# Moving the 1/rms of Q from the softmax scale onto Q itself

## The chip, the cores and the metric

The kernel runs on one core of one Trainium2 chip. The metric is the device time of one execution in microseconds (us). The kernel before takes 629.34 us, the median of three runs (629.11 to 629.71).

A core has five instruction streams that run at once and meet only at semaphores: TensorE (PE, matmuls, with its weight loads PEld), VectorE (DVE), ScalarE (ACT), GpSimd (POOL) and SyncE (SP, which here only issues transfers). Each engine executes its own instructions strictly in the order in which they were queued: an instruction that waits holds everything behind it on the same engine.

## The reference

One layer of a hybrid encoder, 512 tokens of width 2048, all in float32. What matters here is the attention half:

```python
proj = einsum('bsd,de->bse', rms_norm(x, norm_w), w_in)
q, k, v, g_attn, xr, g_lru = split(proj)
q = rms_norm(q.reshape(B, S, 8, 128), q_norm_w)      # per head: q / rms(q) * w
k = rms_norm(k.reshape(B, S, 2, 128), k_norm_w)
q, k = apply_axial_rope(q), apply_axial_rope(k)       # a rotation of pairs of columns
s = (q @ k.T) * 128 ** -0.5                           # per head, 4 query heads share one k
p = softmax(s);  out = p @ v
```

Beside it runs a gated linear recurrence (LRU) over the same tokens. Both halves are normed, gated with silu, joined and multiplied by `w_out`, and the input is added. Since the rotation acts on each token's row linearly, the factor 1/rms of a token and head may be applied before the rotation, after it, or to that token's row of the scores: the result is the same up to rounding.

## The kernel before

Every large product is made of three matmuls (`mm3`, lines 155 to 158): each float32 operand is split into a high part (ACT copies it to a rounded type, `wh`, line 231) and a low part (DVE subtracts, `wl`, line 232), and PE adds high·high, high·low and low·high. A projection goes through `w_in` in chunks of 256 rows by 512 columns (`wload`): SP loads a chunk into a ring of three, ACT and DVE split its two halves, and PE uses the pair for 24 matmuls. `xh` and `xl` hold the split, transposed input.

The order of the stages is: LRU projections and the LRU itself; the projection of K and V with the second half of the LRU; the two projections of Q, four heads each (`both`, `q_proj`, lines 1366 to 1376); then attention (`attention`, line 824), woven into the projections of the gates (`gates`); the last gate; the output projection (`outputs`).

After a Q projection, `evac_tok` (line 645) copies four tiles of 128 tokens by 512 columns out of PSUM, each scaled by the token's input norm. `norm_rope` (line 659) then does, per tile `t`, on ACT four squares with sums (line 670), on POOL the power -1/2 of the mean (`rsqrt_mean`, lines 377 and 378), and on DVE the rotation: two half products with the sines (line 678), the product with the cosines (line 684), the sum (line 685). For K the norm is multiplied in ahead of the rotation (line 676). For Q it is not: the 1/rms values go to a constant table `qscale` of 128 tokens by 2 groups by 4 tiles by 4 heads. `sent` transposes the rotated tiles in blocks on DVE and sends them through DRAM; `landed` and `turned` bring a head back transposed and split it (`q`, line 715).

In the attention, step `i` is head `h = i // 4`, query tile `t = i % 4`. `weights` (line 755) multiplies (scores in a PSUM bank), takes the negated row maximum on DVE (`mx`, line 766), multiplies it by `qscale` on ACT (line 768), exponentiates the scores on ACT with `qscale` as the scale and `mx` as the bias (line 770), takes the reciprocal of the row sums on DVE (line 771), divides on POOL (line 772) and transposes in blocks on DVE (`u`, line 773). Two steps make a half; `moved` sends it through DRAM (lines 781 and 788) and splits what comes back into `ph` (ACT) and `pl` (DVE), both line 792. `values` (line 795) multiplies with V some steps later.

What sets the order: PE's queue is written by hand from line 1222 on (`manual_schedule`), SP's within the attention as well. DVE, ACT and POOL are ordered by a planner at build time: it plays the program through with its own durations and queues, of the instructions ready at that moment, the one with the highest priority; program order is the priority, and `tc.high_priority(AHEAD)` moves the splits of weights and line 768 far ahead. What it queued is fixed on the chip. `STEPS`, `BEGIN` and `LATE` set how many quarters of a chunk PE works on between two steps of the attention.

Of the kernel before, what the change touches and what calls it, by code (L numbers as in the profile page):

```python
# [11 lines left out]
F32 = mybir.dt.float32  # L12
F32R = mybir.dt.float32r
AF = mybir.ActivationFunctionType
# [3 lines left out]
P = 128  # L18
# [3 lines left out]
NT = SEQ // P  # L22
HD = 128
NH = 8
NKV = 2
G = NH // NKV
# [10 lines left out]
AHEAD = 600  # L37
# [22 lines left out]
C_Q, C_K, C_GA, C_XR, C_GL = 0, 1024, 1536, 2560, 3584  # L60
# [6 lines left out]
def hybrid_kernel(  # L67
# [20 lines left out]
    nc = tc.nc  # L88
# [4 lines left out]
    pools, order = {}, {"left": [], "right": []}  # L93
# [27 lines left out]
    def nm(s):  # L121
        cnt[0] += 1
        return f"{s}_{cnt[0]}"
# [10 lines left out]
    def at(tag, bufs, shape, dt=F32):  # L134
        return pools["att"].tile([P, *shape], dt, tag=tag, bufs=bufs, name=nm(tag))
# [10 lines left out]
    def mm():  # L146
        return ps.tile([P, SEQ], F32, tag="mm", name=nm("mm"))

    def const(shape, name, dt=F32):
        return cp.tile(list(shape), dt, tag=name, name=name)  # L150
# [4 lines left out]
    def mm3(acc, lh, ll, rh, rl, start, stop):  # L155
        nc.tensor.matmul(acc, lh, rh, start=start, stop=False)  # L156
        nc.tensor.matmul(acc, lh, rl, start=False, stop=False)  # L157
        nc.tensor.matmul(acc, ll, rh, start=False, stop=stop)  # L158
# [96 lines left out]
    def behind(those):  # L255
        stack = ExitStack()
        for ins in those:
            stack.enter_context(tc.issue_after(ins))
        return stack
# [115 lines left out]
    def rsqrt_mean(dst, src, n, width):  # L375

        nc.gpsimd.tensor_scalar(dst, src, 1.0 / n, EPS, op0=ALU.mult, op1=ALU.add)
        last_pool[0] = nc.gpsimd.tensor_tensor(dst, dst, nhalf[:, :width], op=ALU.pow).ins
# [77 lines left out]
    def proj_tok(c0, acc, early=0):  # L456
        yield from tok_block(acc, w_in, 0, c0, xh, xl, KT, early)
# [7 lines left out]
    def drain(fill):  # L465
        for _ in fill:
            pass
# [177 lines left out]
    def evac_tok(acc, tile_of):  # L645

        res = []
        with tc.high_priority():
            for t in range(NT):
                e = tile_of()  # L650
                evacs[:] = [
                    nc.scalar.activation(e, acc[t], AF.Identity, scale=rstd[:, t : t + 1]).ins
                ]
                res.append(e)
        return res

    qscale = const([P, NKV, NT, G], "qscale")

    def norm_rope(es, nh, tab, home, n="", those=(), scales=()):

        es = [e[:, : nh * HD].rearrange("p (h d) -> p h d", d=HD) for e in es]
        rs = []
        for e in es:
            r = scales.pop(0) if scales else pools[home].tile(
                [P, nh], F32, tag=f"rr{n}", bufs=NT, name=nm("rr")
            )
            for h in range(nh):
                sq = pools[home].tile([P, HD], F32, tag=f"sh{n}", bufs=1, name=nm("sh"))
                with behind(those):
                    nc.scalar.activation(sq, e[:, h, :], AF.Square, accum_out=r[:, h : h + 1])  # L670
            rsqrt_mean(r, r, HD, nh)
            rs.append(r)
        for t, (e, r) in enumerate(zip(es, rs)):
            sq = pools[home].tile([P, nh, HD], F32, tag=f"sq{n}", bufs=2, name=nm("sq"))
            if home == "rope":
                nc.vector.tensor_mul(e, e, r[:, :, None].broadcast_to([P, nh, HD]))
            for s in range(2):
                nc.vector.tensor_mul(
                    sq.rearrange("p h (a s d) -> p h a s d", s=2, d=32)[:, :, :, s, :],
                    e.rearrange("p h (a s d) -> p h a s d", s=2, d=32)[:, :, :, 1 - s, :],  # L680
                    tab[:, t, 1, :].rearrange("p (a s d) -> p a s d", s=2, d=32)[:, None, :, s, :]
                    .broadcast_to([P, nh, 2, 32]),
                )
            nc.vector.tensor_mul(e, e, tab[:, t, 0, :][:, None, :].broadcast_to([P, nh, HD]))
            nc.vector.tensor_add(e, e, sq)
        return es

    kth, ktl = [None] * NKV, [None] * NKV
# [56 lines left out]
    qs = {}  # L745

    def turned(h):

        q = at("q", 2, (2, SEQ), F32R)
        qs[h] = q[:, 0, :], q[:, 1, :]  # L750
        split_head(pairs[h // 2], h % 2, *qs[h])

    pts, summed = {}, []

    def weights(h, t, turned_, first=()):

        (qh, ql), g = qs[h], h // G
        scale = qscale[:, g, t, h % G : h % G + 1]
        tt = slice(t * P, (t + 1) * P)
        sc = mm()  # L760
        mm3(sc, qh[:, tt], ql[:, tt], kth[g], ktl[g], True, True)
        mx, sm = (at(n, 6, (1,)) for n in ("mx", "sm"))
        with ExitStack() as stack:
            for ins in first:
                stack.enter_context(tc.issue_after(ins))
            nc.vector.tensor_reduce(mx, sc, axis=AX.X, op=ALU.max, negate=True)
            with tc.high_priority(AHEAD):
                nc.scalar.activation(mx, mx, AF.Identity, scale=scale)
            p = at("p", 3, (SEQ,))
            nc.scalar.activation(p, sc, AF.Exp, bias=mx, scale=scale, accum_out=sm)  # L770
        nc.vector.reciprocal(sm, sm)  # L771
        last_pool[0] = nc.gpsimd.tensor_scalar(p, p, sm, 0.0, op0=ALU.mult, op1=ALU.add).ins  # L772
        nc.vector.transpose(  # L773
            turned_[:, :, :, t % 2, :].rearrange("p a s c -> p s a c"),
            p.rearrange("p (s a c) -> p s a c", a=NQ, c=B),
        )

    def moved(turned_, half, his):

        aside_ = dram.tile([P, NQ, NT * H // NQ], F32, name=nm("pd"), tag="pd", bufs=2 * NH)  # L780
        nc.sync.dma_start(aside_, turned_.rearrange("p a s t c -> p a (s t c)"))
        yield
        if half == 0:
            his += [at(n, 1, (NT, 2, NQ, H // NQ), F32R) for n in ("ph", "pl")]
        pt = at("pt", 2, (NQ, NT, H // NQ))
        src = aside_.rearrange("(i r) a x -> a r i x", r=B)
        for a in range(NQ):
            nc.sync.dma_start(  # L788
                pt[a * B : (a + 1) * B].rearrange("p i s x -> p i (s x)"), src[a]
            )  # L790
        hi, lo = (v[:, :, half].rearrange("p s i x -> p i s x") for v in his[:2])
        his += [nc.scalar.copy(hi, pt).ins, nc.vector.tensor_sub(lo, pt, f(hi)).ins]  # L792
        yield
# [25 lines left out]
    pairs, rot = [], []  # L819

    def next_pair():
        pairs.append(landed(asides.pop(0)))

    def attention():

        with tc.high_priority(AHEAD):
            for h in range(2):
                turned(h)
        yield BEGIN
        writes = []  # L830
        last, units = NH * NT, {}
        for i in range(last + NT + LATE):
            h, t = divmod(i, NT)
            if i < last:
                if t % 2 == 0:
                    u = at("u", 4, (NQ, NT, 2, B))
                first = pts[h - 2][2 + 2 * t : 4 + 2 * t] if h > 1 and t < 2 else ()
                weights(h, t, u, first)
                if t == 0 and 0 < h < NH - 1:
                    turned(h + 1)  # L840
                if t % 2:
                    units[i] = moved(u, t // 2, pts.setdefault(h, []))
            for j in (i - 1, i - 3):
                if j in units:
                    next(units[j])
            if i < 2:
                es = [e[:, 2 * i : 2 * i + 2] for e in rot]
                writes.append(sent(es, 2, at("u", 4, (NQ, 2, NT, B))))
                next(writes[i])
            elif i < 4:  # L850
                drain(writes[i - 2])
            if t == 2 and h % 2 and asides:
                next_pair()
            j = i - NT - LATE
            if j >= 0 and j % NT == NT - 1:
                hi, lo, *summed[:] = pts.pop(j // NT)
                values(j // NT, hi, lo)
            yield STEPS + (last <= i < last + NT)
# [381 lines left out]
    with tc.high_priority():  # L1240
# [6 lines left out]
        first = []  # L1247
# [103 lines left out]
    rq, rk = rope_consts()  # L1351
# [13 lines left out]
    opened("qkv", "right")  # L1365
    def q_proj(c0, acc):
        yield from proj_tok(c0, acc)
        g = (c0 - C_Q) // (G * HD)
        rot[:] = norm_rope(
            evac_tok(acc, ev), G, rq, "rot", scales=[qscale[:, g, t] for t in range(NT)]  # L1370
        )

    def both():
        yield from q_proj(C_Q, a4)
# [58 lines left out]
    with tc.manual_schedule(engines={mybir.EngineType.SP}):  # L1433
        weave(fill, attention())
# [41 lines left out]
    acc = []  # L1476
# [28 lines left out]
    last = ExitStack()  # L1505
# [47 lines left out]
```

## Time and profile before

| | us |
|---|---|
| median of three runs | 629.34 (629.11 to 629.71) |
| the profiled execution | 629.78 |
| its span, first to last instruction | 628.0 |
| PE busy | 622.1 (99%), 2740 matmuls |
| DVE busy | 490.0 (78%), 778 instructions |
| ACT busy | 370.4 (59%), 678 instructions |
| POOL busy | 106.4 (17%), 141 instructions |

A span of 628.0 us plus 1.78 us around it is the profiled execution's own time. A row of a timeline gives the start (us from the span's start), the duration (us), the engine, the line of the kernel, the operation, what it writes and reads, and, in brackets, the idle time ahead of it with what ended it. A row of a source view gives count and the least, median and greatest duration (ns).

### The profile page before, as it was taken

To read this page: it belongs to the slowest core of one execution; us is meant where nothing else is said; L and a number is where in the kernel's file an instruction comes from. 1 tells how busy PE (TensorE), PEld (TensorE's weight loads), DVE (VectorE), ACT (ScalarE), POOL (GpSimd) and SP (SyncE) were. 2 spreads that over 40 slices of the span, in tenths; PEclk is the share of its full clock that TensorE was granted. 3 is DMA by queue.
4 is the path that set the end of the run, shared out by engine and by line. 5 is a ranking of instruction groups with operands and counts; after the bars stand their busy time and mean duration, and the time that the engine had idled before them with its cause. 6 is when DMAs were issued, how large, how long until landed. Compare 5 with 4: busy or idle time off the path is not lost.

```text
span 628.0 us, 8301 instructions
## 1 busy us (share of the span) xinstructions
PE 622.1 (99%) x2740; PEld 510.9 (81%) x2740; DVE 490.0 (78%) x778; ACT 370.4 (59%) x678; POOL 106.4 (17%) x141
## 2 busy tenths in 40 slices
PE   9999999999999999999999999999999999999997
PEld 7888888888888888888878888888888888888886
DVE  6875878997798957777787888549987865986885
ACT  4586689959964825555585658337445543444441
POOL 3001111112040433621122222100310101101000
PEclk9999999999999999999999999999999999999999
DMA  8999838669765499669659556823995677796442
GB/s 286 317 325 276 208 110 204 141 184 226 200 217 171 111 243 259 155 197 259 190 145 274 176 162 192 251 71 115 269 259 175 218 248 248 251 357 203 134 135 100
DMA packets 75499, 129.72 MB, mean 207 GB/s; under 512 B 6872, under 2 KB 30528, under 8 KB 75456
## 3 DMA queue, kind: packets, MB, share of 16 engines
q1 hardware_dynamic: 67344, 111.70, 56.9%
q0 software_dynamic: 7936, 17.36, 13.8%
q8 instruction: 21, 0.34, 0.2%
q14 instruction: 22, 0.18, 0.1%
q10 hardware_dynamic: 176, 0.14, 0.1%
HBM read 111.34 MB, written 38.80 MB: 239 GB/s over the span
## 4 chain that ended last, share of the span: by engine, by line
PE 97%; DVE 1%; DMA 1%; SPq 0%; issue 0%; POOL 0%; ACT 0%; ACTq 0%; DVEq 0%
PE pj L158 18%; PE pj L157 18%; PE pj L156 18%; PE mm L1100 14%; PE pj L1100 11%; PE mm L157 5%; PE mm L158 5%; PE mm L156 5%; PE pj L421 2%; PE mm L1229 1%; PE mm L266 1%; DMA pt<-pd 1%; SPq L788 0%; DVE pl L792 0%; DVE u L773 0%
## 5 line engine op out<-in xcount | busy, mean ns | idle before, releaser
L231 ACT CAST wh<-wr 128x512 fp32r<-128x512 f32 x142 | 84.5, 618 | 82.3 <-PE pj L157 33.4
L232 DVE TENSOR_TENSOR wl<-wr,wh 128x512 fp32r<-128x512 f32 x144 | 97.6, 705 | 28.7 <-ACT wh L231 25.4
L158 PE MATMUL pj<-x,wl 128*128 128x512 f32 x304 | 118.5, 390 | 0.0
L156 PE MATMUL pj<-x,wh 128*128 128x512 f32 x304 | 118.4, 390 | 0.0
L157 PE MATMUL pj<-x,wh 128*128 128x512 f32 x304 | 118.3, 389 | 0.0
L948 ACT CAST wh<-wr 128x1024 fp32r<-128x1024 f32 (+1 forms) x72 | 60.6, 859 | 78.8 <-PE mm L1100 40.8
L949 DVE TENSOR_TENSOR wl<-wr,wh 128x1024 fp32r<-128x1024 f32 (+1 forms) x72 | 68.8, 985 | 31.9 <-ACT wh L948 31.9
L158 PE MATMUL pj<-wh,x 128*128 128x512 f32 x192 | 74.8, 390 | 0.0
L157 PE MATMUL pj<-wl,x 128*128 128x512 f32 x192 | 74.8, 390 | 0.0
L156 PE MATMUL pj<-wh,x 128*128 128x512 f32 x192 | 74.8, 390 | 0.0
L157 PEld LDWEIGHTS pj<-x,wh 128*128 128x128 f32 x304 | 57.2, 188 | 12.1
L156 PEld LDWEIGHTS pj<-x,wh 128*128 128x128 f32 x304 | 57.1, 188 | 11.9
L158 PEld LDWEIGHTS pj<-x,wl 128*128 128x128 f32 x304 | 57.1, 188 | 11.9
L972 POOL DMA_DIRECT2D t<-in_w_out_dram x40 | 33.4, 906 | 132.9 <-DMA t<-in_w_out_dram 75.5
L1100 PE MATMUL mm<-wh,mh 128*128 128x512 f32 x126 | 49.4, 392 | 0.0
L1100 PE MATMUL mm<-wl,mh 128*128 128x512 f32 x126 | 49.4, 392 | 0.0
L1100 PE MATMUL mm<-wh,ml 128*128 128x512 f32 x126 | 49.4, 392 | 0.0
L156 PEld LDWEIGHTS pj<-wh,x 128*128 128x128 f32 x192 | 36.0, 188 | 7.7
L157 PEld LDWEIGHTS pj<-wl,x 128*128 128x128 f32 x192 | 36.1, 188 | 7.6
L158 PEld LDWEIGHTS pj<-wh,x 128*128 128x128 f32 x192 | 36.0, 188 | 7.5
L772 POOL TENSOR_SCALAR p<-p,sm 128x512 f32<-128x512 f32 x32 | 23.7, 740 | 93.5 <-DVE sm L771 93.5
L1100 PE MATMUL pj<-wl,mh 128*128 128x512 f32 (+1 forms) x100 | 38.8, 388 | 0.0
(231 smaller groups left out, 1181.2 us busy)
## 6 DMA issues: line engine op xcount, KB each, us to landing
wr<-in_w_in_dram SPq DMA_DIRECT2D x71, 512.0 KB, 4.9
wr<-in_w_out_dram SPq DMA_DIRECT2D x21, 512.0 KB, 6.4
t<-in_w_out_dram POOLq DMA_DIRECT2D x40, 256.0 KB, 7.0
wr<-t SPq DMA_DIRECT2D x40, 256.0 KB, 5.4
pd<-u SPq DMA_DIRECT2D x16, 512.0 KB, 3.0
pt<-pd SPq DMA_DIRECT2D x64, 128.0 KB, 3.7
t<-in_w_out_dram SPq DMA_DIRECT2D x24, 256.0 KB, 4.9
wr<-in_w_out_dram SPq DMA_DIRECT2D x22, 256.0 KB, 5.0
```

What stands on the lines that cost most here:

```text
L156: nc.tensor.matmul(acc, lh, rh, start=start, stop=False)
L157: nc.tensor.matmul(acc, lh, rl, start=False, stop=False)
L158: nc.tensor.matmul(acc, ll, rh, start=False, stop=stop)
L231: copy(hi, raw[:, k, :]).ins,
L232: nc.vector.tensor_sub(lo, raw[:, k, :], f(hi)).ins,
L266: nc.tensor.transpose(pt[:, t * P : (t + 1) * P], xc[:, t, ks], ident)
L421: nc.tensor.matmul(acc[e], w[:, e * P : (e + 1) * P], x_[2 * c + k], start=c == k == j == 0, stop=False,)
L772: last_pool[0] = nc.gpsimd.tensor_scalar(p, p, sm, 0.0, op0=ALU.mult, op1=ALU.add).ins
L948: nc.scalar.copy(hi[:, to], b)
L949: nc.vector.tensor_sub(lo[:, to], b, f(hi[:, to]))
L972: nc.gpsimd.dma_start(dst, src, accum_op=ALU.add)
L1100: nc.tensor.matmul(dst[s][:, es], lh[:, ts_], rh[:, es], start=i == ends_[0] and j == 0, stop=i == ends_[1] and j == 2,)
```

## The change

The table `qscale` goes. The 1/rms of Q is held in small tiles `rr` of the pool `rot`, and each rotated tile of Q is multiplied by it on DVE behind the sum of the rotation: eight products of 128 by 512, one per tile of each projection. In the attention the scaling of the maximum on ACT goes (32 instructions), and the exponential takes no scale. For K the order stays as it was.

```diff
-    qscale = const([P, NKV, NT, G], "qscale")
-
-    def norm_rope(es, nh, tab, home, n="", those=(), scales=()):
+    def norm_rope(es, nh, tab, home, n="", those=(), last=False):
...
-            r = scales.pop(0) if scales else pools[home].tile(
-                [P, nh], F32, tag=f"rr{n}", bufs=NT, name=nm("rr")
-            )
+            r = pools[home].tile([P, nh], F32, tag=f"rr{n}", bufs=NT, name=nm("rr"))
...
-            if home == "rope":
+            if not last:
                 nc.vector.tensor_mul(e, e, r[:, :, None].broadcast_to([P, nh, HD]))
...
             nc.vector.tensor_add(e, e, sq)
+            if last:
+                nc.vector.tensor_mul(e, e, r[:, :, None].broadcast_to([P, nh, HD]))
...
-    def weights(h, t, turned_, first=()):
-        (qh, ql), g = qs[h], h // G
-        scale = qscale[:, g, t, h % G : h % G + 1]
+    def weights(q, g, t, turned_, first=()):
+        qh, ql = q
...
             nc.vector.tensor_reduce(mx, sc, axis=AX.X, op=ALU.max, negate=True)
-            with tc.high_priority(AHEAD):
-                nc.scalar.activation(mx, mx, AF.Identity, scale=scale)
             p = at("p", 3, (SEQ,))
-            nc.scalar.activation(p, sc, AF.Exp, bias=mx, scale=scale, accum_out=sm)
+            nc.scalar.activation(p, sc, AF.Exp, bias=mx, accum_out=sm)
...
-                weights(h, t, u, first)
+                weights(qs[h], h // G, t, u, first)
...
     def q_proj(c0, acc):
         yield from proj_tok(c0, acc)
-        g = (c0 - C_Q) // (G * HD)
-        rot[:] = norm_rope(
-            evac_tok(acc, ev), G, rq, "rot", scales=[qscale[:, g, t] for t in range(NT)]
-        )
+        rot[:] = norm_rope(evac_tok(acc, ev), G, rq, "rot", last=True)
```

## Prediction, made before the changed kernel was run

> **What bounds the kernel now.** I read the page first: the busy shares and the chain that ended last.
>
> ```profile
> PE 622.1 (99%) x2740; PEld 510.9 (81%) x2740; DVE 490.0 (78%) x778; ACT 370.4 (59%) x678; POOL 106.4 (17%) x141
> PE 97%; DVE 1%; DMA 1%; SPq 0%; issue 0%; POOL 0%; ACT 0%; ACTq 0%; DVEq 0%
> ```
>
> PE is busy for all but 6 us of the span and holds 97% of the chain. A busy PE can still be a slow one, so next come the waits of PE and a stretch of the table by windows (PE, PEld, DVE, ACT, POOL busy with counts, then clock and DMA).
>
> ```profile
> PE mm L157 <- DVE pl L792: 1.1, 1, 1.1
> ```
>
> ```profile
> 335.00:400.00 65.00, 65.00 (x287) 53.74 (x286) 51.08 (x83) 41.77 (x81) 16.56 (x19) 1.00 0.67 197
> ```
>
> Inside the kernel PE waits for DVE once, for 1.1 us, at a `pl`. In a stretch without a wait it starts a matmul every 65.00 / 287 = 0.226 us at the full clock (no more than that, since some records can be missing). The change leaves PE's queue as it is: the same matmuls in the same order. So the time can change only where PE stands still: that one wait can shrink, and new waits can come. The start and the end of the kernel lie outside of what the edit touches.
>
> The one wait is followed back by the timelines of PE, DVE and ACT:
>
> ```profile
> 307.13 0.68 DVE L766 TENSOR_REDUCE mx<-mm 128x1 f32<-128x512 f32 x1
> 307.85 0.29 ACT L768 ACTIVATE mx<-mx,qscale 128x1 f32<-128x1 f32 x1 [2.03 <-DVE mx L766]
> 308.24 0.78 ACT L770 ACTIVATE p<-mm,mx,qscale 128x512 f32<-128x512 f32 x1
> 310.13 0.71 DVE L773 STREAM_TRANSPOSE u<-p 128x512 f32<-128x512 f32 x1 [0.83 <-POOL p L772]
> 310.76 1.18 DVE L792 TENSOR_TENSOR pl<-pt,ph 128x1024 fp32r<-128x1024 f32 x1
> 311.87 0.68 DVE L766 TENSOR_REDUCE mx<-mm 128x1 f32<-128x512 f32 x1
> 312.58 0.29 ACT L768 ACTIVATE mx<-mx,qscale 128x1 f32<-128x1 f32 x1 [1.50 <-DVE mx L766]
> 312.97 0.78 ACT L770 ACTIVATE p<-mm,mx,qscale 128x512 f32<-128x512 f32 x1
> 313.74 1.04 ACT L792 CAST ph<-pt 128x1024 fp32r<-128x1024 f32 x1
> 314.86 0.71 DVE L773 STREAM_TRANSPOSE u<-p 128x512 f32<-128x512 f32 x1 [0.82 <-POOL p L772]
> 315.50 1.18 DVE L792 TENSOR_TENSOR pl<-pt,ph 128x1024 fp32r<-128x1024 f32 x1
> 315.26 0.39 PE L156 MATMUL mm<-ph,v 128*128 128x512 f32 x1
> 316.74 0.50 PE L157 MATMUL mm<-pl,v 128*128 128x512 f32 x1 [1.09 <-DVE pl L792]
> ```
>
> From below: PE starts head 1's product with V at 315.26 and gets its second matmul, the first to read `pl`, off at 316.74. Against 0.23 us for a normal step that is a stall of 316.74 - 315.26 - 0.23 = 1.25 us. `pl` starts at 315.50, although its ACT part `ph` is done at 313.74 + 1.04 = 314.78: it stands in DVE's queue behind a transpose that waits 0.82 us for POOL, which waits for the exponential of 312.97, which stands behind line 768, which waits for the row maximum of 311.87. And that maximum stands in the queue behind the `pl` of 310.76, behind the transpose of 310.13, behind the previous step's exponential of 308.24, line 768 of 307.85 and maximum of 307.13. So two softmax steps lie one after the other on the path that ends in the stall, and line 768 is in each.
>
> **The change, part by part.** The operations it adds and removes:
>
> ```profile
> L684 DVE TENSOR_TENSOR ev<-ev,rq x8: 650/684/693, 203.8 to 257.8; 128x512 f32<-128x512 f32 x8
> L676 DVE TENSOR_TENSOR kv<-kv,rr x4: 417/418/418, 183.4 to 191.4; 128x256 f32<-128x256 f32 x4
> L768 ACT ACTIVATE mx<-mx,qscale x32: 278/295/301, 265.8 to 389.8; 128x1 f32<-128x1 f32 x32
> L231 ACT CAST wh<-wr 128x512 fp32r<-128x512 f32 x142 | 84.5, 618 | 82.3 <-PE pj L157 33.4
> ```
>
> *Removed: 32 scalings of the maximum (line 768).* Busy time: 32 × 0.295 = 9.4 us of ACT, whose idle time costs nothing. On the path, a step loses the time from line 768's start to the exponential's: 308.24 - 307.85 = 0.39 us and 312.97 - 312.58 = 0.39 us. The exponential then waits for the maximum itself, as line 768 does now (2.03 and 1.50 us in its brackets), so no wait is new on ACT and the same instructions stand behind it. Nothing else on this path becomes late: `ph` follows the exponential on ACT and moves with it, from an end of 314.78 to 314.00, and `pl` would start at 314.72. Sum: 0.78 us off the stall of 1.25, which leaves 0.47.
>
> *Changed: the exponential takes no scale from memory.* The trace has no such exponential. Above, its 0.78 us of now; below, the 0.62 us of the cast of line 231, a 128x512 on ACT without a scale. I take 0.78, since it is the same function on the same PSUM tile; the other end would be worth 2 × 0.16 = 0.32 us more on this path, still less than the stall that is left.
>
> *Added: eight products of 128x512 on DVE.* The nearest row is line 684, a 128x512 product with an operand repeated over the heads: 0.684 us (0.650 to 0.693). Line 676 is the same product by r as the new one, at half the width: 0.418 us, so the way r is repeated costs nothing extra. Eight make 5.5 us of DVE, four for each projection of Q. Do they reach PE? The stretches where they go, and where the work displaced by them can go:
>
> ```profile
> 203.00:222.00 19.00, 19.00 (x85) 15.75 (x84) 18.56 (x33) 15.06 (x45) 10.10 (x11) 1.00 0.47 124
> 222.00:240.00 18.00, 18.00 (x80) 14.75 (x80) 6.77 (x12) 4.44 (x8) 5.11 (x7) 1.00 1.04 263
> 249.70:262.20 12.50, 12.50 (x57) 10.34 (x56) 12.21 (x24) 7.82 (x28) 8.19 (x9) 1.00 0.52 102
> 262.20:264.90 2.70, 2.70 (x14) 2.22 (x13) 0.04 (x1) 0.00 (x0) 1.32 (x2) 1.00 1.07 272
> ```
>
> For the first four, DVE has 19.00 - 18.56 = 0.44 us free while 2.74 us come in, and 11.2 us free in the 18 us behind. For the second four, 0.29 us free in the first stretch and 2.66 us in the one behind. So work shifts back by up to 2.7 us, and the question is whether splits of weights, which PE needs, are in it. What the new product waits for is r, POOL's power:
>
> ```profile
> 204.57 0.69 DVE L685 TENSOR_TENSOR ev<-ev,sq 128x512 f32<-128x512 f32 x1
> 205.71 0.69 DVE L232 TENSOR_TENSOR wl<-wr,wh 128x512 fp32r<-128x512 f32 x1
> 206.65 0.68 DVE L232 TENSOR_TENSOR wl<-wr,wh 128x512 fp32r<-128x512 f32 x1
> 204.68 1.45 POOL L378 TENSOR_TENSOR qscale<-qscale,nhalf 128x4 f32<-128x4 f32 x1
> L685 DVE TENSOR_TENSOR ev<-ev,sq x8: 652/684/694, 204.6 to 259.0; 128x512 f32<-128x512 f32 x8
> L378 POOL TENSOR_TENSOR qscale<-qscale,nhalf x8: 1331/1332/1453, 204.7 to 255.9; 128x4 f32<-128x4 f32 x8
> ```
>
> In the first tile the sum ends at 204.57 + 0.69 = 205.26 and r at 204.68 + 1.45 = 206.13: if the planner queues the product straight behind the sum, DVE stands for 0.87 us, and the split of 205.71 and everything behind it wait. In the last tile r is there at 255.9 + 1.33 = 257.2, ahead of the sum (259.0 + 0.68); I count one such wait. Its price: 0.87 + 0.68 = 1.55 us on splits that end at 206.65 + 0.68 = 207.33. PE takes that pair of splits up when seven pairs of 24 matmuls are still to come before the gates (248.98 below): 248.98 - 7 × 24 × 0.226 = 211.0. The cover is 3.7 us, so the cost is nothing; if the cover were gone, it would be the 1.55.
>
> For the second four, the tightest splits are those that end at 257.90 and 259.10:
>
> ```profile
> 248.98 0.40 PE L156 MATMUL pj<-x,wh 128*128 128x512 f32 x1
> 257.22 0.68 DVE L232 TENSOR_TENSOR wl<-wr,wh 128x512 fp32r<-128x512 f32 x1
> 258.42 0.68 DVE L232 TENSOR_TENSOR wl<-wr,wh 128x512 fp32r<-128x512 f32 x1
> ```
>
> PE starts the gates at 248.98 and takes the third pair up at 248.98 + 48 × 0.226 = 259.8, its second half three matmuls later, at 260.5. The covers are 1.9 and 1.4 us. At most three of the new products can be queued ahead of them (the sum of the fourth tile comes behind): 2.05 us, so between 0 and 2.05 - 1.4 = 0.65 us of stall. I take 0: splits rank far ahead of the rotation in the planner's order, so an added product pushes other products back rather than a split, and the idle 2.66 us follow. Behind the products come the block transposes of Q and the transfers to DRAM. The second group's come in the attention only, 10 us later. The first group's are issued by SP among the loads of weights, which a late transfer holds up by the same 2.7 us at most, and behind it the loads do run late:
>
> ```profile
> 221.71 0.34 SPq L302 DMA_DIRECT2D qd<-uq  x1
> 239.51 0.62 ACT L231 CAST wh<-wr 128x512 fp32r<-128x512 f32 x1 [6.32 <-DMA wr<-in_w_in_dram]
> ```
>
> The cast that waits longest for a load is the one of 239.51. It serves the gates from 248.98 on, 9.5 us later, less 0.7 for the low part; 2.7 us fit in, and the price is nothing again.
>
> *The constants.* 128 bytes a partition fewer, and the small tiles of r instead. No row shows a cost of an address; the two bounds are zero, since no instruction is added by it.
>
> **The sum.** The profiled execution is 628.0 + 1.78 = 629.78 us, 0.44 above the median of the runs. 629.78 - 0.78 = 629.00; on the scale of the median, 629.34 - 0.78 = 628.56. Its own range is 628.1 (the whole stall gone, 629.34 - 1.25) to 629.3.
>
> **Rivals.**
>
> *The stall goes altogether.* The planner lays DVE's queue out anew with shorter steps; if `pl` comes ahead of the transpose that waits, the 0.47 go too. For it: `ph` is done 0.72 us before `pl` starts. Against: a planner places what is ready, and it placed the transpose first. 628.1 us, a shade under the 0.2% (1.26 us) which I take for what a measurement of this kernel can tell from no change.
>
> *No net gain.* The stall shrinks by 0.78 and the split above comes 0.65 late: 629.2 us. For it: the small cover. Against: the rank of the splits.
>
> *`pl` falls behind one more softmax step (slower).* The heads next to the stalled one have hardly any cover either:
>
> ```profile
> 297.49 1.18 DVE L792 TENSOR_TENSOR pl<-pt,ph 128x1024 fp32r<-128x1024 f32 x1
> 299.08 0.39 PE L157 MATMUL mm<-pl,v 128*128 128x512 f32 x1
> 332.01 1.19 DVE L792 TENSOR_TENSOR pl<-pt,ph 128x1024 fp32r<-128x1024 f32 x1
> 333.29 0.46 PE L157 MATMUL mm<-pl,v 128*128 128x512 f32 x1
> ```
>
> Head 0's `pl` ends at 298.67 for a matmul at 299.08, head 2's at 333.20 for 333.29: covers of 0.41 and 0.09 us. With ACT instructions gone the planner's clock runs differently, and it can queue one more step (maximum, reciprocal, waiting transpose) ahead of a `pl`. Such a step took from 311.87 to 315.50, 3.63 us, of which two splits of 0.68 would have run anyway: 2.27 us. It decides from the cover on: 2.27 - 0.09 = 2.18 us for one head, 628.56 + 2.18 = 630.7; for two heads 632.9. For it: the covers. Against: every step is 0.39 us shorter, which gives each head cover.
>
> *DVE becomes the bound from 203 to 222 (slower).* 18.56 + 2.74 + 0.87 = 22.17 us of work in 19.00: 3.17 us over. If PE had to wait for all of it, 628.56 + 3.17 = 631.7. Against: the 11.2 free us behind, and the cover of 3.7 us. The Trainium skill, Perfetto Trace Analysis, section Optimizing Scalar/DVE Operations, speaks for this rival: where DVE is saturated, it says, work should go to ScalarE, and this edit takes work from ScalarE and gives it to a DVE that is 98% busy there. By that rule the time would be this rival's; that PE has no wait in that stretch now although DVE is full bears rather on the cover than on the rule.
>
> **How the numbers follow.** Forecast 0.40, stall gone 0.21, no net gain 0.15, `pl` behind a step 0.17, DVE the bound 0.07. Faster by over 0.2%: only from the stall gone and something small beside it, 0.13 of its 0.21. Slower: the last two, 0.24. Same: 0.40 + 0.08 + 0.15 = 0.63. The predicted time is the forecast's, 628.6. The range goes down to 627.9 (the stall gone and the 0.2 us by which the runs scatter) and up to 631.2, past one head's step; it leaves out two heads and the full DVE case, about 0.13, and little below.
>
> **What would show it.** Right: PE's wait for `pl` near 315 at 0.3 to 0.5 us instead of 1.1; the exponential about 0.04 us behind the end of the maximum; line 768 gone and ACT about 9 us less busy; DVE about 5.5 us more; eight products near 0.68 us, the first of them with a wait for POOL of up to 0.9; no wait of PE for `wl`. Wrong: PE waiting for `pl` in several heads, or for `wl` near 211 or 260, or a count of waits that no step above names.

## The result and the profile after

The changed kernel takes 624.97 us (median; 624.81 to 625.17) against 629.52 us of the kernel before in the same session: a ratio of 0.9929, 95% interval 0.9912 to 0.9946. That is 4.5 us faster. The forecast was 628.6, with a range that began at 627.9: the direction was right, the size was not. The profiled execution took 625.17 us, its span 623.2.

The page of the changed kernel, busy shares and shares of the chain that ended last:

```profile
PE 618.4 (99%) x2740; PEld 511.1 (82%) x2740; DVE 495.4 (79%) x786; ACT 359.6 (58%) x646; POOL 107.4 (17%) x141
PE 99%; DVE 0%; issue 0%
```

PE has the same 2740 matmuls, but 618.4 us of busy time where it had 622.1. So 3.7 us went out of time in which PE counted as *busy*, and only the rest out of waits. The wait for `pl` is gone; what is left of waits between the start and the end of the kernel is mainly one late split of weights, in the waits of PE's weight loads (PEld):

```profile
PEld pj L158 <- DVE wl L232: 0.4, 1, 0.4
```

Where did busy time go? The chain in order of time shows the output projection in groups of twelve matmuls. First the kernel before (start, duration, what):

```profile
469.22 2.72 PE mm L1100 x12
471.95 2.79 PE pj L1100 x12
474.74 2.80 PE mm L1100 x12
```

Then the changed kernel, the same three groups:

```profile
466.75 2.72 PE mm L1095 x12
469.48 2.72 PE pj L1095 x12
472.19 2.72 PE mm L1095 x12
```

Twelve matmuls took 2.72 us in the first of these groups of the kernel before and 2.79 to 2.80 in the next two; after the change each group takes 2.72. The same in the mean of a group of instructions, before and after (count, busy us, mean ns):

```profile
L1100 PE MATMUL mm<-wh,mh 128*128 128x512 f32 x126 | 49.4, 392 | 0.0
```

```profile
L1095 PE MATMUL mm<-wh,mh 128*128 128x512 f32 x126 | 49.0, 389 | 0.0
```

And in the windows of 135 us in the output projection (PE's count is in the first bracket):

```profile
475.00:610.00 135.00, 135.00 (x587) 110.00 (x587) 104.50 (x131) 59.19 (x73) 11.55 (x18) 1.00 0.66 222
```

```profile
475.00:610.00 135.00, 135.00 (x597) 111.74 (x596) 106.59 (x133) 59.77 (x74) 11.54 (x18) 1.00 0.67 220
```

PE is 100% busy in both, at a granted clock of 1.00, and gets through 587 matmuls in the one and 597 in the other. A busy share cannot show this; counts per microsecond do.

The softmax path to the place of the old stall, from the timelines of DVE, ACT and PE of the changed kernel:

```profile
304.71 0.69 DVE L763 TENSOR_REDUCE mx<-mm 128x1 f32<-128x512 f32 x1
305.31 1.29 DVE L232 TENSOR_TENSOR wl<-wr,wh 128x512 fp32r<-128x512 f32 x2
305.49 0.69 ACT L765 ACTIVATE p<-mm,mx 128x512 f32<-128x512 f32 x1 [0.17 <-DVE mx L763]
306.51 0.69 DVE L713 TENSOR_TENSOR q<-lq,q 128x512 fp32r<-128x512 f32 x1
307.12 0.16 DVE L766 RECIPROCAL sm<-sm 128x1 f32<-128x1 f32 x1
308.11 0.71 DVE L768 STREAM_TRANSPOSE u<-p 128x512 f32<-128x512 f32 x1 [0.83 <-POOL p L767]
308.74 1.18 DVE L787 TENSOR_TENSOR pl<-pt,ph 128x1024 fp32r<-128x1024 f32 x1
309.85 0.68 DVE L763 TENSOR_REDUCE mx<-mm 128x1 f32<-128x512 f32 x1
310.45 1.28 DVE L232 TENSOR_TENSOR wl<-wr,wh 128x512 fp32r<-128x512 f32 x2
310.62 0.69 ACT L765 ACTIVATE p<-mm,mx 128x512 f32<-128x512 f32 x1 [0.76 <-DVE mx L763]
311.30 1.04 ACT L787 CAST ph<-pt 128x1024 fp32r<-128x1024 f32 x1
312.63 0.71 DVE L768 STREAM_TRANSPOSE u<-p 128x512 f32<-128x512 f32 x1 [0.83 <-POOL p L767]
313.27 1.18 DVE L787 TENSOR_TENSOR pl<-pt,ph 128x1024 fp32r<-128x1024 f32 x1
314.71 0.39 PE L156 MATMUL mm<-ph,v 128*128 128x512 f32 x1
314.93 0.39 PE L157 MATMUL mm<-pl,v 128*128 128x512 f32 x1
```

`pl` ends at 313.27 + 1.18 = 314.45, and PE reads it at 314.93, in step.

The new and changed instructions, from the source views (the exponential; the product with r, and what DVE waited for ahead of it; the dots mark lines left out):

```profile
L765 ACT ACTIVATE p<-mm,mx x32: 674/687/692, 267.0 to 387.5; 128x512 f32<-128x512 f32 x32
...
L683 DVE TENSOR_TENSOR ev<-ev,rr x8: 648/690/693, 206.0 to 262.5; 128x512 f32<-128x512 f32 x8
  POOL rr L378: 0.9, 1
```

### The profile page after: what moved, and what is told of

It reads as the page before. It is cut to its first block, busy times and chain, and to the rows that moved or that the text cites. A ratio compares the mean times of both kernels' runs of the same rounds, so it can differ in the third digit from the quotient of the medians.

```text
span 623.2 us, 8296 instructions
## 1 busy us (share of the span) xinstructions
PE 618.4 (99%) x2740; PEld 511.1 (82%) x2740; DVE 495.4 (79%) x786; ACT 359.6 (58%) x646; POOL 107.4 (17%) x141
## 4 chain that ended last, share of the span: by engine, by line
PE 99%; DVE 0%; issue 0%
PE pj L158 19%; PE pj L157 19%; PE pj L156 19%; PE mm L1095 14%; PE pj L1095 11%; PE mm L156 5%; PE mm L158 5%; PE mm L157 5%; PE pj L421 2%; PE mm L1224 1%; PE mm L266 1%; PE mm L891 0%; DVE cb L1124 0%; PE mm L200 0%; PE pj L399 0%
## 5 line engine op out<-in xcount | busy, mean ns | idle before, releaser
L232 DVE TENSOR_TENSOR wl<-wr,wh 128x512 fp32r<-128x512 f32 x144 | 99.3, 714 | 28.1 <-ACT wh L231 26.2
L1095 PE MATMUL pj<-wh,mh 128*128 128x512 f32 (+1 forms) x100 | 38.5, 385 | 0.0
```

The lines of the kernel that those rows point to most:

```text
L232: nc.vector.tensor_sub(lo, raw[:, k, :], f(hi)).ins,
L1095: nc.tensor.matmul(dst[s][:, es], lh[:, ts_], rh[:, es], start=i == ends_[0] and j == 0, stop=i == ends_[1] and j == 2,)
```

## What lies behind it: the places of the operands

The edit of the arithmetic leaves PE's queue untouched, but it takes a table of 128 bytes a partition out of the pool of constants, which lies at the bottom of the left side of the memory. Everything on the left above it moves down by 128 bytes; what is allocated from the right end stays. In the built programs the tiles start at these places:

| tiles | side | start, modulo 256 bytes, before | after |
|---|---|---|---|
| split input `x`, splits of weights `wh`, `wl` (pools xw, out), `mh`, `ml` in out | left | 64 | 192 |
| splits in pools wx and fin, `q`, `kt`, `v`, `ph`, `pl`, `mh`, `ml` in fin and hq, the LRU's tiles | right | 192 | 192 |

A matmul has two operands in this memory, one streamed through the engine and one loaded into it ahead of that (the weight load). Since trace and program both hold 2740 matmuls in one order, each step from one start to the next can be put beside the places of its operands. I count full matmuls of 512 columns behind 20 us, and steps below 260 ns, so that stalls are out. *Mixed*: the two operands start differently modulo 256. *Change*: they start alike, but the next matmul's do not start like them. *Rest*: all alike. The last column is the sum of what lies over 226.7 ns a step.

| kernel | mixed: steps, mean ns | change | rest | over 226.7 ns, us |
|---|---|---|---|---|
| before | 363, 232.7 | 118, 231.4 | 2148, 227.2 | 3.8 |
| changed | 3, 236.0 | 3, 225.7 | 2626, 226.7 | 0.0 |
| 1: changed, 128 bytes put back | 363, 232.7 | 118, 231.5 | 2151, 227.2 | 3.8 |
| 2: before, left side moved | 3, 236.0 | 3, 225.7 | 2624, 226.7 | 0.1 |
| 3: before, right side moved | 3, 236.0 | 3, 225.7 | 2620, 226.7 | 0.2 |
| 4: changed, one pool moved | 339, 233.0 | 20, 227.7 | 2275, 226.8 | 2.4 |
| 5: changed, left side by 64 | 363, 230.6 | 118, 227.4 | 2151, 227.8 | 4.0 |
| 6: changed, left side by 192 | 362, 232.9 | 118, 227.9 | 2152, 228.1 | 5.3 |

In the kernel before a mixed matmul costs 6 ns more in the mean, and a change of sides nearly 5. Of the 363 mixed ones 324 are in the output projection. The rest pays a little too, 227.2 ns: 1.1 of the 3.8 us. All of that lies in the first ten steps behind a mixed matmul or a change, which take 227.9 ns in the mean; further on it is 226.7. That was a theory from one pair of traces; the rival was that the new arithmetic and the new order of the engines had done it in a way that the profile does not name. Experiments 1 to 6 move tiles without touching an instruction.

## The experiments

The runs of experiments 1 to 4 share a session in which the kernel before took 629.84 us, those of 5 to 8 one in which it took 629.81. Ratios are to the kernel before of the same session.

**1. The changed kernel with the 128 bytes put back**

```diff
+    const([P, 32], "gap")
     def norm_rope(es, nh, tab, home, n="", those=(), last=False):
```

> The changed kernel with an unused tile of 128 bytes a partition among the constants, where the table of scales stood; every engine's instructions and their order are those of the changed kernel, and the tiles of the left side lie where they lay before the change. Theory (place of the matmul operands): the left side starts at 64 bytes past a multiple of 256, the right side at 192; matmuls that take one operand from each side go at 232 to 233 ns instead of 227, and those at a change of sides lose about as much: 3.8 us more than the changed kernel, 628.8 us, PE busy through with no wait for pl. Rival (the edit of the arithmetic and the new order of the engines): as the changed kernel, 625.0 us.

Measured: 628.51 us, ratio 0.9980 (0.9971 to 0.9989). PE has no wait for `pl`. Its chain at the start of the output projection:

```profile
468.39 2.72 PE mm L1097 x12
471.11 2.79 PE pj L1097 x12
```

The pace of the kernel before is back, and with it, by the ratios, (0.9980 - 0.9929) × 629.5 = 3.2 us. The arithmetic alone is worth 629.84 - 628.51 = 1.3 us, which is where the forecast's own range ended.

**2. The kernel before with its left side moved**

```diff
     qscale = const([P, NKV, NT, G], "qscale")
+    const([P, 32], "gap")
```

> The kernel before with 128 unused bytes more among the constants, the order of all engines unchanged. Left and right side then lie alike, both 192 bytes past a multiple of 256. Theory (place): a steady 227 ns a matmul in the output stage too, 3.8 us less than before, 625.7 us, with PE's wait of about 1.1 us for pl still there near 315. Rival (arithmetic and order): 629.5 us as before.

Measured: 626.41 us, ratio 0.9946 (0.9934 to 0.9959): 3.4 us faster with not one instruction changed. Its chain, and its wait:

```profile
468.01 2.72 PE mm L1101 x12
470.73 2.72 PE pj L1101 x12
```

```profile
PE mm L157 <- DVE pl L793: 1.2, 1, 1.2
```

The pace is the changed kernel's, the stall is the old kernel's.

**3. The kernel before with its right side moved**

```diff
-    opened("pad", "right").tile([P, 8], F32, name="pad")
+    opened("pad", "right").tile([P, 40], F32, name="pad")
```

> The kernel before with the unused tile at the end of the right side made 128 bytes larger: the right side moves down to 64 bytes past a multiple of 256, where the left side lies in the kernel before; the left side stays. Theory (what counts is how the two operands lie to each other): 625.7 us, as with the left side moved. Rival (the place of the left side alone counts): 629.5 us. Rival (arithmetic and order): 629.5 us.

Measured: 626.29 us, ratio 0.9944 (0.9932 to 0.9957), with the wait of 1.2 us in place:

```profile
PE mm L157 <- DVE pl L792: 1.2, 1, 1.2
```

Here both sides start at 64, where the left side was slow before. So neither place is slow by itself; what counts is how the two lie to each other.

**4. The changed kernel with one pool moved**

```diff
-        + [([P, 4, H], "t4", 2)]
+        + [([P, 4, H], "t4", 2), ([P, 32], "gap", 1)]
     ):
         pools["fin"].tile(shape, F32, tag=tag, bufs=bufs, name=nm(tag))
```

> The changed kernel with 128 unused bytes at the end of the pool fin, which serves the last gate and the output projection: only fin's tiles move, to 64 bytes past a multiple of 256; the order is unchanged. Theory (place): up to the output projection a steady 227 ns a matmul as in the changed kernel, then 232 to 233 where one operand is of fin and the other of the pool out or of the ring: 2.4 us more, 627.4 us, all of it behind 466 us. Rival (arithmetic and order): 625.0 us.

Measured: 627.68 us, ratio 0.9962 (0.9950 to 0.9975), by the ratios 2.1 us over the changed kernel (2.4 by the sum of the steps). Two windows, one in the attention and one in the output projection:

```profile
335.00:400.00 65.00, 65.00 (x288) 53.84 (x287) 48.83 (x80) 35.61 (x64) 15.95 (x17) 1.00 0.69 204
475.00:610.00 135.00, 135.00 (x588) 110.06 (x587) 105.44 (x132) 59.31 (x73) 11.54 (x18) 1.00 0.67 222
```

In the second there are 588 matmuls in 135 us, as in the kernel before (587) and not as in the changed kernel (597). In the first the counts are too close to tell (287 before, 289 changed, 288 here), but the mean step is not: 226.7 ns as in the changed kernel, against 227.6 before. The cost goes where the mixed operands go.

**5 and 6. Differences of 64 bytes**

```diff
+    const([P, 16], "gap")        # 5
+    const([P, 48], "gap")        # 6
     def norm_rope(es, nh, tab, home, n="", those=(), last=False):
```

> The changed kernel with 64 unused bytes among the constants: the left side starts at 0 past a multiple of 256, the right side at 192, 64 bytes apart and in the other half of the 256. Theory A (what counts is the half of 256 bytes, 128 each, in which the operands start): as with 128 bytes, mixed matmuls at 232 to 233 ns, 3.5 us more than the changed kernel, 628.5 us. Theory B (only a distance of 128 costs, 64 is free): 625.0 us. Theory C (each difference costs by its size): between, near 626.8 us.

> The changed kernel with 192 unused bytes among the constants: the left side starts at 128 past a multiple of 256, the right side at 192, again 64 bytes apart, but in the same half of the 256. Theory A (half of the 256 bytes): no mixed matmul loses, 625.0 us. Theory B (only a distance of 128 costs): 625.0 us. Theory C (each difference costs): as the kernel with 64 unused bytes, near 626.8 us or more.

Measured: 628.80 us, ratio 0.9985 (0.9976 to 0.9994), and 630.04 us, ratio 1.0003 (0.9994 to 1.0012). The output projection in 5 and in 6:

```profile
475.00:610.00 135.00, 135.00 (x591) 110.52 (x590) 106.35 (x133) 60.59 (x75) 11.52 (x18) 1.00 0.67 222
```

```profile
475.00:610.00 135.00, 135.00 (x587) 109.64 (x586) 104.24 (x130) 59.36 (x73) 11.52 (x18) 1.00 0.67 222
```

Theories A and B fall: 6 has its operands in the same half of the 256 bytes and no distance of 128, and is the slowest of all. C holds in its first half, every difference tried costs; in its second, that the cost goes by the size of the difference, it falls, since 64 bytes apart cost as much as 128 in sum one way and more the other (4.0 and 5.3 us in the table's last column, 3.8 for 128). The sums are made up otherwise, though: a mixed matmul costs less in 5 (230.6 ns) and as much in 6 (232.9) as 128 bytes apart, and the *rest* is slower (227.8 and 228.1 ns). Again that lies in the first ten steps behind a mixed matmul or a change, 229.4 ns in 5 and 230.0 in 6; further on it is 226.7 in both, as in every other kernel of the table.

These experiments move whole sides or a whole pool, and with them the tiles of the other engines. That it is the operands of the matmuls which count is read from the table, where the cost stands at and shortly behind the mixed and changing steps and nowhere else; no run moved the operands alone.

**7. The changed kernel with ACT's step put back**

```diff
+            with tc.high_priority(AHEAD):
+                nc.scalar.activation(mx, mx, AF.Identity, scale=ones[:, :1])
             p = at("p", 3, (SEQ,))
-            nc.scalar.activation(p, sc, AF.Exp, bias=mx, accum_out=sm)
+            nc.scalar.activation(p, sc, AF.Exp, bias=mx, scale=ones[:, :1], accum_out=sm)
```

> The changed kernel, all its tiles in their places, with ACT's step put back by a scale of ones: the maximum is multiplied by 1 on ACT ahead of the exponential, which takes the scale from memory again. Q is scaled on DVE as in the changed kernel. Theory (the ACT step taken off the softmax path is what ended PE's wait for pl): the wait near 315 comes back with about 1.1 us, the exponential takes 0.78 us instead of 0.69, 626.3 us. Rival (the new order of DVE behind the products ended it): no wait, 625.0 us.

Measured: 627.32 us, ratio 0.9963 (0.9951 to 0.9976), by the ratios 2.1 us over the changed kernel. Its runs scatter from 626.18 to 628.69, as widely as those of 5 (627.91 to 630.12) and more than those of the other experiments, and why they do is open. The profiled execution is the one of 626.18, 1.0 us over the changed kernel's. Its wait, the two instructions on ACT (busy us, mean ns), and the place of the maximum on DVE:

```profile
PE mm L157 <- DVE pl L789: 1.2, 1, 1.2
```

```profile
L767 ACT ACTIVATE p<-mm,mx,ones 128x512 f32<-128x512 f32 x32 | 24.9, 778 | 1.7
L765 ACT ACTIVATE mx<-mx,ones 128x1 f32<-128x1 f32 x32 | 9.3, 292 | 28.1 <-DVE mx L763 27.9
```

```profile
305.06 1.25 DVE L232 TENSOR_TENSOR wl<-wr,wh 128x512 fp32r<-128x512 f32 x2
306.23 0.68 DVE L763 TENSOR_REDUCE mx<-mm 128x1 f32<-128x512 f32 x1
```

The stall returns with the ACT step, although DVE keeps the products. So it was what the change took off ACT, with the order that the planner then gives, and not the products on DVE, that ended it. The run puts the step and the scale of the exponential back together and does not tell them apart. The stall of 1.2 us accounts for the profiled execution; what more the median of 2.1 us holds is open.

**8. The changed kernel without the products**

```diff
-            if last:
-                nc.vector.tensor_mul(e, e, r[:, :, None].broadcast_to([P, nh, HD]))
```

> The changed kernel without the eight products of Q by 1/rms: it leaves Q's normalisation out. Theory (the products are hidden behind PE's work): 0.3 us less at most, since the late split near 255 that stops PE for 0.3 us should come in time, 624.7 to 625.0 us. Rival (DVE pays for them on the path): 2 us less or more, 623 us.

Without the products the kernel leaves the normalisation of Q out. Measured: 624.54 us, ratio 0.9919 (0.9906 to 0.9933), which the intervals do not tell from the changed kernel's. Its busy shares:

```profile
PE 617.8 (99%) x2740; PEld 510.6 (82%) x2740; DVE 490.4 (79%) x778; ACT 359.5 (58%) x646; POOL 106.4 (17%) x141
```

That is 618.4 - 617.8 = 0.6 us less of PE's busy time, with no wait for a split of weights and none for `pl`. So the eight products, 5.5 us of DVE, cost half a microsecond or so by these profiles, which the times alone do not tell from nothing.

## Why the prediction was wrong

**The step that failed** stands in two places. "The change leaves PE's queue as it is", and "so the time can change only where PE stands still": it can also change in how long PE takes for the same matmul. And on the constants: "No row shows a cost of an address; the two bounds are zero, since no instruction is added by it." What 128 bytes did, experiments 2 and 3 measured: 3.4 and 3.6 us, three quarters of the gain. The rows were in the profile of before: groups of twelve at 2.72 and at 2.79 to 2.80 us stand one below the other in its chain. The working took the pace of one stretch, 0.226 us, for the pace of all and then asked only for gaps. The Trainium skill warns of it (Perfetto Trace Analysis, Identifying the Most-Contended Engine): how busy the matmuls are is no good measure of how near TensorE is to its limit, the share of peak arithmetic reached and the busy share of the weight loads are better ones. On the first the trace agrees: the matmuls are 99% busy in both kernels. The share of the weight loads does not tell the two apart here: the same loads (510.9 and 511.1 us) went from 81% to 82% of the span, but experiment 1, at the slow pace, has 82% as well (511.6 us of 627.2).

**The stall.** The forecast took 0.78 us off 1.25 and left 0.47. All of it went, but not in the way that was forecast. The steps did become shorter on ACT: the exponential starts 310.62 - 309.85 - 0.68 = 0.09 us behind the end of the maximum (0.04 said) and not 312.97 - 311.87 - 0.68 = 0.42, and without a scale it takes 0.687 us and not 0.78; the bound that was written down and not chosen, 0.62, was nearer, and experiment 7, with the scale, has 0.778. Yet the path of two steps did not become shorter. From the start of its first maximum to the start of the last `pl` it took 315.50 - 307.13 = 8.37 us before and 313.27 - 304.71 = 8.56 after. In its first step the exponential is done early, but the reciprocal now stands in DVE's queue behind two splits of weights and one of Q and starts only at 307.12. What ended the stall is that this path starts 307.13 - 304.71 = 2.42 us earlier, while PE comes to the product only 315.26 - 314.71 = 0.55 us earlier. Before, the maximum of step 11 stood behind a transpose that waits for POOL and two splits of weights:

```profile
305.33 0.71 DVE L773 STREAM_TRANSPOSE u<-p 128x512 f32<-128x512 f32 x1 [0.83 <-POOL p L772]
305.96 1.25 DVE L232 TENSOR_TENSOR wl<-wr,wh 128x512 fp32r<-128x512 f32 x2
307.13 0.68 DVE L766 TENSOR_REDUCE mx<-mm 128x1 f32<-128x512 f32 x1
```

After the change the planner puts it ahead of the splits, and in experiment 7, where the stall is back, behind them again. So the term of 0.78 us came out on ACT, nearly, and not on the path: the order on DVE decided. The rival "the stall goes altogether", which had 0.21 and 628.1 us, named a new order of DVE, but another one: `pl` still stands behind the transpose that waits 0.83 us. With the places put back (experiment 1) the ratio is 0.9980, which on the median of before makes 629.34 × 0.9980 = 628.1 us: that rival's time, with the forecast's 628.6 inside the interval. That the arithmetic alone comes so near the forecast is in part luck.

**The products on DVE.** Eight at 0.684 us in the mean, as costed. One wait for r of 0.9 us (0.87 said), in the first tile. Where the displaced work went, in the windows of the changed kernel:

```profile
203.00:222.00 19.00, 19.00 (x86) 15.73 (x85) 18.07 (x32) 14.93 (x44) 9.13 (x11) 1.00 0.42 120
222.00:240.00 18.00, 18.00 (x81) 14.91 (x80) 9.36 (x18) 3.95 (x7) 4.75 (x6) 1.00 1.02 243
```

DVE does 18.07 us in the full stretch and 9.36 where it did 6.77: 2.6 us moved into the free time behind, and PE did not wait there. The rival "DVE becomes the bound" came to nothing, since idle time followed within 20 us. The Trainium skill (Perfetto Trace Analysis, Optimizing Scalar/DVE Operations) says that with a saturated DVE, offloading some work to ScalarE may make sense; here the opposite step, into a stretch where DVE was busy for 18.56 of 19.00 us before, made PE wait nowhere in it.

In the second group a late split was foreseen, at one pair's distance from the truth: not the third pair but the second. Its second half was the tightest in the kernel before already, which the working missed: it ended at 253.28 + 0.68 = 253.96 and was read at 255.58, 1.6 us of cover against 2.4 and 1.9 for the halves of the third pair, counted the same way. It now starts 1.17 us later, 0.61 of them for the product of the first tile.

```profile
254.45 0.68 DVE L232 TENSOR_TENSOR wl<-wr,wh 128x512 fp32r<-128x512 f32 x1
254.77 0.39 PE L157 MATMUL pj<-x,wh 128*128 128x512 f32 x1
255.19 0.50 PE L158 MATMUL pj<-x,wl 128*128 128x512 f32 x1
```

The split ends at 254.45 + 0.68 = 255.13, and the matmul that reads it starts 0.42 us after the last one instead of 0.23: 0.2 us lost, and about 0.1 in the next step. The forecast had given it 0 to 0.65 and took 0.

**ACT and DVE in sum.** ACT is 10.8 us less busy. By their own rows line 768 gave 9.3 and the shorter exponential 3.0; these add up to more, since the busy share counts time in which two records overlap once, and ACT's other groups took 0.5 longer. DVE is 5.4 us more busy (5.5 said).

**`pl` behind one more step.** It did not happen, and no head waits. But the shorter steps did not give every head cover, as the argument against that rival said: from the end of the last `pl` to the matmul that reads it, head 0 went from 0.4 to 1.2 us and head 2 from 0.1 to only 0.2, and the last four heads lost up to 0.6.

## What to carry to other kernels

An edit that adds or drops a tile moves its neighbours, so a change can pay or cost by a few bytes of padding alone; where a result does not fit the working, run the old kernel with the new places before explaining anything else. On an engine that is busy all the time, read the pace (instructions per microsecond, or equal groups in the chain) by stretches: a busy share hides it. And where a stage draws its two matmul operands from two allocation sides, make them start alike modulo 256 bytes; here that was worth 3.4 us for 128 unused bytes a partition.

## What the runs showed of the hardware that I had not expected

A matmul of 512 columns in the rounded 32-bit type goes at a steady 226.7 ns from start to start where streamed and loaded operand start alike modulo 256 bytes, whether both at 64 or both at 192. Where they start 128 bytes apart, it takes 232.7 ns in the mean, and a change from one place to the other between two matmuls costs about 5 ns. Up to ten matmuls behind either are slower as well, by 1.2 ns in the mean. With starts 64 bytes apart a mixed matmul takes 230.6 ns (left side at 0, right at 192) or 232.9 (left at 128, right at 192). A difference of 256 bytes costs nothing: in the changed kernel the two sides start at 192 and 448 modulo 512. The granted clock was 1.00 in all these stretches. What in the chip does it, and what other distances or smaller matmuls cost, is open: only starts 64, 128 and 256 bytes apart were tried.
